# A two-layer hybrid transformer kernel: an order that counts TensorE's instructions, inverse, scan and projections recorded in turns, fewer live tiles, first loads issued at once

## The chip, the cores and the metric

The kernel runs on one core of a Trainium2 chip. A core has five engines that each take their instructions in order: TensorE (PE in the profile; its weight loads are PEld), VectorE (DVE), ScalarE (ACT), GpSimd (POOL) and SyncE (SP), which here issues all DMAs. The metric is device microseconds from the first to the last instruction, as the median of repeated runs; lower is better.

## What is computed

Two layers work on a context stream and a main stream of 256 tokens each, width 1024. Cut to what matters here:

```python
for l in range(2):
    mod = silu(c) @ w_ada[l] + b_ada[l]
    h   = rms_norm(x) * (1 + sc1) + sh1
    q, k, v, z, b, a, u, vg, p, gate = split(h @ w_in[l])
    q, k, v = silu(conv5(q, k, v))
    # per head, direction and chunk: m = strict_lower(beta k k^T decay)
    # sol = (I + m)^-1 rhs ; then a scan over chunks carries the state s
    y_a = norm(o) * silu(z)
    x = x + g1 * (sum(gate_i * (y_i @ w_br_i)) @ w_out)
    x = x + g2 * expert_choice_ffn(rms_norm(x) * (1 + sc2) + sh2)
return rms_norm(x)
```

Eight heads, two directions, both streams; the context's result starts the main stream's scan. The feed-forward part has 16 experts; its weights alone are 192 transfers of 1 MiB in each layer.

## The kernel before, in words

**Recording and ordering.** The program is not written in the order in which it runs. `Net.record` (line 713) calls methods that record operations with their dependences into a `Prog`; `Prog.order` (line 377) then lays them on the engines with a list scheduler, and `emit` (line 609) writes them out. That is why every instruction of the profile carries line 628. Operations are taken by priority (the place in the recording, shifted by `bias`), and only within a window `win` ahead of the oldest one not yet started. `place` (line 407) gives each tile room in one of 25 pages of 2048 words per partition; `give` (line 461) takes it back. `run` (line 701) sets `limits`, the number of tiles of a kind that may live at once (`w` weights as loaded, `hi` their split halves, `wa` modulation weights, `we` expert weights).

**TensorE's two queues.** In the loop of `order` (from line 528 on) matmuls that fill only part of the array (`op.part`) wait in a queue of their own, `ready["tile"]`. That queue goes first if its head is older than the head of the other and full-size matmuls have filled at least `share` of the planner's last `clock` nanoseconds, and once a group is begun (`group[2]`) it goes on first.

**The mixing stage.** `gdn` (line 971) goes over four head pairs `j`. `heads_in` projects, convolves and normalizes k, v and q; `heads_solve` (line 1230) makes the products of keys with decays for both streams (`products`, line 1238) and inverts the chunk matrices (`inverse`, line 1383); `heads_scan` (line 1280) runs the scan. `inverse` works on 32x32 blocks: eight dependent steps (four levels of two) of 64 small matmuls each, then steps for 32 and 64 columns, with a VectorE operation behind each step. A matmul of fp32 operands becomes two matmul instructions and two weight loads, so a step of 64 is 128 of each. `products` loads rows of decays broadcast over the partitions (`rows`), three for a main-stream half, into tiles `R`. Projections (`proj`, line 925) and the other branches (`side`, line 1554) use split operands (fp32r high and low parts, `wsplit`, line 903) and depend little on the scan; `take(n)` records the next `n` of them between solve and scan, as `FILL` says. `Y` and `X64` hold the inverse's result, two sets of each (`NY`).

**The rest.** `ada_in` (line 873) makes the first modulation from 16 weight tiles; the streams are loaded by `record` (line 713), the context first, the main stream after six of the modulation's steps (`XAT`). `merge` and `route` (lines 1591, 1640) end the mixing; `moe` and `expert` (lines 1732, 1782) stream the expert weights.

Of the kernel before, what the change touches and what calls it, by code (L numbers as in the profile page):

```python
# [257 lines left out]
class Prog:  # L258
# [21 lines left out]
    def record(s, eng, fn, a, k):  # L280
# [42 lines left out]
        lim = a[0].tile.lim if isinstance(a[0], View) else None  # L323
        if (not op.deps or eng[0] == "dma") and lim not in ("w", "wa", "we"):
            op.win = min(op.win, 400)
        if lim in ("w", "wa", "we"):
            op.win = 10 ** 9
# [49 lines left out]
    def order(s):  # L377
# [29 lines left out]
        def place(t, spare):  # L407

            up = (t.last - t.first) > 1500 or t.size < 256
            al = 1 << (t.size - 1).bit_length()  # L410
            dt = F32R if t.dt == F32R else F32
            cls = (up, max(al, 256))
            order = range(PAGES - 1, -1, -1) if up else range(PAGES)
            if t.lim == "we":
                order = sorted(order, key=lambda i: freed[i])
            for step in range(3):
                if step == 1 and sum(g is None for g in pages) <= spare:
                    continue
                for i in order:
                    g = pages[i]  # L420
                    if (g is None) != (step == 1) or (g is not None and (g.dt != dt or (step == 0 and g.cls != cls))):
# [39 lines left out]
        def give(t, addr):  # L461
            if t.space == "psum":
                free_banks.append(addr)
                return
            page, a = addr
            b, hs = a + t.size, holes[page.i]
            j = bisect.bisect(hs, (a, b))
            hs.insert(j, (a, b))
            if j + 1 < len(hs) and hs[j + 1][0] == b:
                hs[j:j + 2] = [(a, hs[j + 1][1])]  # L470
            if j > 0 and hs[j - 1][1] == a:
                hs[j - 1:j + 1] = [(hs[j - 1][0], hs[j][1])]
            if hs[0] == (0, PAGE):
                pages[page.i] = None
                turn[0] += 1
                freed[page.i] = turn[0]

# [32 lines left out]
        while left:  # L510
# [17 lines left out]
            for e in engines:  # L528
# [3 lines left out]
                if e == "pe":  # L532
# [3 lines left out]
                    if ready["tile"]:  # L536
                        while recent and recent[0][0] < now - clock:
                            recent.pop(0)
                        much = not span[3] or sum(r[1] for r in recent) < s.limits["share"] * clock
                        queues.append(ready["tile"])  # L540
                        x = ready["tile"][0]
                        if ready[e] and (x < ready[e][0] and not much or group[2]):
                            queues.reverse()
                aside, tries = [], 0
                while queues:
# [26 lines left out]
                    if e == "pe":  # L572
# [57 lines left out]

XAT = 6
CALLS = (-3, -1)
# [24 lines left out]
class Net:  # L657
# [43 lines left out]
    def run(s):  # L701
        tc, t = s.tc, s.t
        limits = dict(w=4, hi=5, wa=5, we=18, fill=0.94, window=800, spare=0, clock=4096 / 1.2, share=0.5, room=ROOM)
        with tc.tile_pool(name="sb", bufs=1) as sb, tc.tile_pool(name="ps", bufs=1, space=PSUM) as ps, \
# [8 lines left out]
    def record(s):  # L713
# [25 lines left out]
        s.xin = [p.tile([128, 2, D], F32, name="xin") for _ in range(2)]  # L739
        nc.sync.dma_start(s.xin[0], s.rows[0].rearrange("(t p) d -> p t d", p=128))  # L740
        s.small = {}
# [10 lines left out]
        for n, _ in enumerate(s.ada_in(0)):  # L752
            if n == EAT:
                s.mark = len(p.ops)
            if n == XAT:
                nc.sync.dma_start(s.xin[1], s.rows[1].rearrange("(t p) d -> p t d", p=128))
        p.bias = LATE
# [115 lines left out]
    def ada_in(s, l):  # L873

        nc, t = s.nc, s.t
        for hf in range(2):
            ps = s.bank("ada")
            for kt in range(8):
                w = s.p.tile([128, 2, 512], F32, name="wada", lim="wa")
                nc.sync.dma_start(w.rearrange("p a b -> p (a b)"), t["w_ada"][l, 0, hf, kt])  # L880
# [90 lines left out]
    def gdn(s, l, ms, side):  # L971
# [21 lines left out]
        take(3)  # L993
        sol = s.heads_solve(ms, 0, qkv[0], Y[0], X[0])
        take(FILL[0])
        for j in range(4):
            p.win = WIN[1]
            o, S, now = {}, None, sol
            for m in ms:
                o[m.k], S = s.heads_scan(m, j, qkv[j][m.k], now[m.k], S)  # L1000
                take(FILL[1])
                if j < 3 and m is ms[0]:
                    sol = s.heads_solve(ms, j + 1, qkv[j + 1], Y[(j + 1) % NY], X[(j + 1) % NY])
                    take(FILL[2])
            while j not in zs:
# [123 lines left out]
    def conv_silu(s, l, units, blk, out):  # L1129
# [3 lines left out]
        for v, bs in units:  # L1133
# [3 lines left out]
            for b in range(nb):  # L1137
# [3 lines left out]
                for tap in (0, 1, 3, 4):  # L1141
# [3 lines left out]
                                             st(acc)[:, :, lo:hi], op0=ALU.mult, op1=ALU.add)  # L1145
                th = s.p.tile([128, n], F32, name="th")
                s.act(th, acc, AF.Tanh, scale=0.5)
# [81 lines left out]

    def heads_solve(s, ms, j, qkv, Y, XF):  # L1230


        MT = [s.p.tile([128, 8, 128], F32, name="MT") for d in range(2)]
        part = {m.k: s.products(m, j, qkv[m.k], [a[:, 4 * z:4 * z + 4, :] for a in MT]) for z, m in enumerate(ms)}
        s.inverse(MT, Y, XF)
        return {m.k: (Y[:, :, 4 * z:4 * z + 4, :],) + part[m.k] for z, m in enumerate(ms)}

    def products(s, m, j, qkv, MT):
# [9 lines left out]
        for i in range(2):  # L1248
            ts = slice(128 * i, 128 * i + 128)
            R = []  # L1250
            for kind in range(3):
                r = None
                if full or kind != 1:
                    r = s.p.tile(B4, F32, name="R")
                    nc.sync.dma_start(r.rearrange("p d h c -> p (d h) c"),
                                      s.bc_rows(s.rowsd[l][k], (kind * 16 + 4 * j) * 256 + 128 * i, [[256, 4], [1, 128]]))
                R.append(r)
# [5 lines left out]
            E = s.p.tile(B4, F32, name="E")  # L1263
            s.tt(E, R[0], s.nb[:, :, None, :].to_broadcast(B4), ALU.add)
# [3 lines left out]
            Eb = s.p.tile(B4, F32, name="Eb")  # L1268
            s.tt(Eb, E, R[2], ALU.mult)
            for d in range(2):  # L1270
                s.tt(MT[d][:, 2 * i:2 * i + 2, :], kq[:, 0], Eb[:, d], ALU.mult)
            if full:
                s.tt(attn[:, i], kq[:, 1][:, None].to_broadcast(B4), E, ALU.mult)
                s.tt(qt[:, i], R[1], qT[:, None, :, ts].to_broadcast(B4), ALU.mult)
        return attn, qt
# [3 lines left out]

    def heads_scan(s, m, j, qkv, sol, S):  # L1280
        nc, k, full, cl = s.nc, m.k, m.full, m.cl
# [9 lines left out]
        for n in range(2):  # L1291
# [38 lines left out]
            if k == 1 and n == 1:  # L1330
                break
            sp2 = s.bank("sp").rearrange("p (d h c) -> p d h c", d=2, h=2)
# [6 lines left out]
            else:  # L1339
                sd = s.p.tile(B4, F32, name="sd")  # L1340
                for d in range(2):
# [4 lines left out]
            S = S2  # L1346
        return o, S

# [34 lines left out]
    def inverse(s, MT, Y, XF):  # L1383
# [21 lines left out]
        for lv in range(1, 5):  # L1405
# [13 lines left out]
            YT = s.p.tile(C4, F32, name="Yc")  # L1419
            V.transpose(flat(YT), flat(X))  # L1420
        for q in range(4):
            s.p.av.copy(units16(Y)[Q[q], :, 32 * q:32 * q + 32], units16(YT)[Q[q]])
# [22 lines left out]
        V.transpose(line(XF[Q[1], 0]), line(yc[Q[0]]))  # L1445
        V.transpose(line(XF[Q[2], 1]), line(yc[Q[3]]))

        H = (slice(0, 64), slice(64, 128))
# [10 lines left out]
        V.tensor_copy(Y[H[0], 0, :, 64:128], yy[H[0]])  # L1459
        V.tensor_copy(Y[H[1], 1, :, 0:64], yy[H[1]])  # L1460

    def chunk_mlp(s, l, ms, rng, yb):
# [390 lines left out]
```

## Time and profile before

| | us |
|---|---|
| median of 3 runs (2397.95 to 2399.71) | 2399.62 |
| the profiled execution, its own time | 2393.84 |
| span of its profile | 2392.1 |
| PE busy in the span | 2041.2 |
| DVE busy | 1122.6 |
| ACT busy | 686.3 |

Busy time is time in which at least one instruction of the engine runs. PEclk (granted clock) is a share of TensorE's full speed: 1.0 is 2.4 GHz, 0.5 is 1.2 GHz. The span falls into a mixing stage (to about 870 us), the experts of layer 0 (to 1312), mixing of layer 1 (to about 1990) and its experts.

### The profile page before, as it was taken

What the parts mean: (1) busy time and instruction counts of PE and PEld (TensorE: products, weight loads), DVE (VectorE), ACT (ScalarE), POOL (GpSimd) and SP (SyncE); (2) the same over time, 40 slices, a digit from 0 to 9 for tenths busy, and PEclk for the clock granted to TensorE, in tenths of its full rate; (3) what the DMA queues carried; (4) which work ended last, traced back from release to release, by engine and by line L of the source; (5) the groups of instructions that cost most, each with busy time, mean ns of one, the idle gap of its engine ahead of it and who ended that gap; (6) DMA issues with size and microseconds to landing.
All of it is one profiled execution on the core that took longest, in us unless ns stands there. A gap on an engine that the chain in (4) does not pass through costs nothing.

```text
span 2392.1 us, 49338 instructions
## 1 busy us (share of the span) xinstructions
PE 2041.2 (85%) x21357; PEld 1344.3 (56%) x21357; DVE 1122.6 (47%) x2478; ACT 686.3 (29%) x1466; POOL 49.3 (2%) x41
## 2 busy tenths in 40 slices
PE   7999989799999989878787899988799976666665
PEld 4877868698779843222222477777799932121111
DVE  4978767664236732212121787666775521010102
ACT  4544436243224420000000455444554410000000
POOL 0000000000000210000000000000000010000000
PEclk9999999899999999999999999898999988887888
DMA  8523314233346599999999743432436989999997
GB/s 292 167 80 110 108 64 138 78 117 106 132 155 232 194 342 421 421 421 421 421 422 421 291 143 119 153 90 69 130 107 214 337 331 421 421 421 421 421 421 308
DMA packets 153906, 602.95 MB, mean 252 GB/s; under 512 B 13948, under 2 KB 60092, under 8 KB 104536
## 3 DMA queue, kind: packets, MB, share of 16 engines
q1 hardware_dynamic: 153688, 599.80, 65.7%
q8 instruction: 167, 2.74, 0.5%
q14 instruction: 51, 0.42, 0.1%
HBM read 597.45 MB, written 2.29 MB: 251 GB/s over the span
## 4 chain that ended last, share of the span: by engine, by line
PE 49%; DMA 36%; DVE 9%; issue 4%; ACT 2%; SPq 0%; DVEq 0%; ACTq 0%
PE bank L628 49%; DMA page<-in_w_up_dram 19%; DMA page<-in_w_down_dram 10%; DVE page L628 9%; DMA page<-in_w_gate_dram 3%; ACT page L628 2%; DMA page<-in_w_in_dram 1%; DMA page<-rows 1%; DMA page<-in_w_ada_dram 1%; DMA page<-in_n_dram 0%; SPq L628 0%; DMA page<-in_b_ada_dram 0%; ACT L628 0%; DVEq L1849 0%; DVEq L628 0%
## 5 line engine op out<-in xcount | busy, mean ns | idle before, releaser
L628 PE MATMUL bank<-page,page 32*32 32x32 f32 (+8 forms) x20611 | 2024.4, 322 | 338.0 <-DVE page L628 99.0
L628 PEld LDWEIGHTS bank<-page,page 32*32 32x32 f32 (+5 forms) x20611 | 1321.4, 143 | 1031.5 <-issue 398.8
L628 ACT ACTIVATE page<-page 128x1024 fp32r<-128x1024 f32 (+7 forms) x485 | 341.4, 719 | 499.3 <-PE bank L628 244.7
L628 DVE TENSOR_TENSOR page<-page,page 128x1024 fp32r<-128x1024 f32 (+3 forms) x471 | 401.5, 876 | 151.7 <-ACT page L628 128.4
L628 ACT ACTIVATE page<-bank 128x512 f32<-128x512 f32 (+5 forms) x332 | 160.2, 497 | 1062.4 <-PE bank L628 1046.4
L628 DVE TENSOR_TENSOR page<-page,bank 128x512 f32<-128x512 f32 (+2 forms) x152 | 96.6, 644 | 578.8 <-ACT page L628 265.7
L628 DVE TENSOR_TENSOR page<-bank,page 128x512 f32<-128x512 f32 (+4 forms) x286 | 147.7, 530 | 283.8 <-PE bank L628 280.5
L628 ACT ACTIVATE page<-page,page 128x128 f32<-128x128 f32 (+2 forms) x388 | 143.9, 435 | 48.4 <-DVE page L628 41.0
L628 DVE SCALAR_TENSOR_TENSOR page<-page,page,page 128x508 f32<-128x508 f32 (+4 forms) x188 | 107.8, 595 | 1.2
L628 DVE COPY page<-bank 128x512 f32<-128x512 f32 (+7 forms) x100 | 52.6, 527 | 36.9 <-PE bank L628 35.4
L628 DVE SCALAR_TENSOR_TENSOR page<-page,page 128x512 f32<-128x512 f32 (+5 forms) x93 | 65.2, 706 | 9.5 <-DMA page<-in_n_dram 7.4
L628 ACT ACTIVATE page<-bank,page 128x256 f32<-128x256 f32 (+2 forms) x85 | 42.0, 516 | 83.3 <-PE bank L628 64.7
L628 DVE SCALAR_TENSOR_TENSOR page<-page,bank 128x512 f32<-128x512 f32 x48 | 32.8, 684 | 60.5 <-PE bank L628 58.4
L628 POOL TENSOR_TENSOR page<-page,page 128x512 fp32r<-128x512 f32 (+1 forms) x16 | 21.2, 1351 | 1915.6 <-ACT page L628 1465.9
L628 DVE TENSOR_SCALAR page<-bank,page 128x128 f32<-128x128 f32 (+3 forms) x65 | 31.2, 496 | 54.5 <-PE bank L628 44.9
L628 DVE TENSOR_TENSOR page<-page 128x4 f32<-128x4 f32 (+3 forms) x301 | 55.2, 197 | 3.3 <-issue 0.3
L628 DVE TENSOR_SCALAR page<-page 128x4 f32<-128x4 f32 (+7 forms) x216 | 37.5, 187 | 25.4 <-ACT page L628 15.6
L628 PE MATMUL bank<-page 32*32 32x32 f32 (+2 forms) x746 | 37.8, 225 | 1.8 <-issue 1.8
L628 DVE TENSOR_SCALAR page<-page,page 128x128 f32<-128x128 f32 (+2 forms) x120 | 37.0, 338 | 2.8 <-PE bank L628 2.0
L628 DVE STREAM_TRANSPOSE page<-page 128x512 f32<-128x512 f32 (+1 forms) x56 | 35.2, 629 | 1.2 <-PE bank L628 0.4
L628 DVE SCALAR_TENSOR_TENSOR page<-bank,page,page 128x128 f32<-128x128 f32 x96 | 29.2, 343 | 10.0 <-PE bank L628 9.9
L628 PEld LDWEIGHTS bank<-page 32*32 32x32 f32 (+2 forms) x746 | 31.1, 133 | 4.4 <-issue 3.2
(23 smaller groups left out, 163.2 us busy)
## 6 DMA issues: line engine op xcount, KB each, us to landing
page<-in_w_gate_dram SPq DMA_DIRECT2D x128, 1024.0 KB, 19.8
page<-in_w_up_dram SPq DMA_DIRECT2D x128, 1024.0 KB, 19.8
page<-in_w_down_dram SPq DMA_DIRECT2D x128, 1024.0 KB, 19.8
page<-in_w_in_dram SPq DMA_DIRECT2D x136, 512.0 KB, 3.9
page<-in_w_ada_dram SPq DMA_DIRECT2D x96, 512.0 KB, 5.3
page<-rows SPq DMA_DIRECT2D x88, 256.0 KB, 5.1
page<-in_w_br_a_dram SPq DMA_DIRECT2D x24, 512.0 KB, 3.6
page<-in_w_out_dram SPq DMA_DIRECT2D x24, 512.0 KB, 4.8
```

The lines of the kernel that those rows point to most:

```text
L628: op.inst = getattr(eng[op.on], fn)(*a, **k)
```

## The change

Five things change. (1) `order` keeps a count of instructions that TensorE may still take before its supply is refilled: `fetch` starts at 320, each operation takes 2 (4 if `op.part`), and 256 come back in 3700 ns of the planner's time. A group of part-array matmuls is begun only when the count is at 250 or more. (2) `gdn` records solve, scan and projections in turns by the string `TURNS`; `heads_solve`, `scans` and `inverse` become generators. (3) Fewer tiles: the decay rows are loaded straight into `E`, `Eb` and `qt`, `th` and `sd` reuse other tiles, `Y` and `X64` have one set (`NY = 1`), `w`, `hi` and `wa` may have 3, 4 and 4 live tiles. (4) `place` goes through the pages of short-lived tiles in the order in which room in them was last given back, and takes an empty page as readily as a partly used one while more than 8 are empty. (5) The 16 first modulation weights get a kind of their own (`wi`, limit 16), and the two streams are loaded after three and seven steps.

```diff
@@ place, give
-            if t.lim == "we":
+            empty = sum(g is None for g in pages)
+            if not up:
                 order = sorted(order, key=lambda i: freed[i])
-            for step in range(3):
-                if step == 1 and sum(g is None for g in pages) <= spare:
+            for step in range(0 if up or empty <= ROOMY else -1, 3):
+                if step == 1 and empty <= spare:
...
@@ order
+        fetch = [CREDIT, 0.0]
...
-                        if ready[e] and (x < ready[e][0] and not much or group[2]):
+                        if group[2]:
+                            fed = fetch[0] + (now - fetch[1]) * REFILL > 0
+                        else:
+                            fed = fetch[0] + (now - fetch[1]) * REFILL >= START
+                        if ready[e] and fed and (x < ready[e][0] and not much or group[2]):
                             queues.reverse()
...
+                        fetch[0] = min(CREDIT, fetch[0] + (now - fetch[1]) * REFILL) - (4 if op.part else 2)
+                        fetch[1] = now
+                        c += max(0.0, -fetch[0] / REFILL)
...
-XAT = 6
+ROOMY = 8
+CREDIT, REFILL, START = 320.0, 256 / 3700.0, 250.0
+XAT = (3, 7)
-FILL = (6, 1, 2)
+FILL = (1,)
+TURNS = ("bsbspbsbsbpbpbpb", "sspssp")
-NY = 2
+NY = 1
-        limits = dict(w=4, hi=5, wa=5, we=18, ...
+        limits = dict(w=3, hi=4, wa=4, wi=16, we=18, ...
@@ gdn
-        sol = s.heads_solve(ms, 0, qkv[0], Y[0], X[0])
-        take(FILL[0])
+        sol = {}
+        for _ in s.heads_solve(ms, 0, qkv[0], Y[0], X[0], sol):
+            take(FILL[0])
         for j in range(4):
             p.win = WIN[1]
-            o, S, now = {}, None, sol
-            for m in ms:
-                o[m.k], S = s.heads_scan(m, j, qkv[j][m.k], now[m.k], S)
-                take(FILL[1])
-                if j < 3 and m is ms[0]:
-                    sol = s.heads_solve(ms, j + 1, qkv[j + 1], Y[(j + 1) % NY], X[(j + 1) % NY])
-                    take(FILL[2])
+            o, now, sol = {}, sol, {}
+            while j < 3 and len(qkv.get(j + 1, ())) < len(ms):
+                take(1)
+            scan = s.scans(ms, j, qkv[j], now, o)
+            solve = s.heads_solve(ms, j + 1, qkv[j + 1], Y[(j + 1) % NY], X[(j + 1) % NY], sol) if j < 3 else iter(())
+            for c in TURNS[j > 2]:
+                if c == "p":
+                    take(1)
+                else:
+                    next(scan if c == "s" else solve, None)
...
@@ products
-            R = []
-            for kind in range(3):
...
+            E, Eb = s.p.tile(B4, F32, name="E"), s.p.tile(B4, F32, name="Eb")
+            for kind, r in enumerate((E, qt[:, i] if full else None, Eb)):
+                if r is not None:
...
-            s.tt(Eb, E, R[2], ALU.mult)
+            s.tt(Eb, E, Eb, ALU.mult)
```

In the orders below a row is a run of equal instructions, out<-in and the output's shape; page and bank numbers only tell tiles apart.

TensorE in the inverse of the second head pair, layer 0: each 32x32 row pair or x64 row is one step of 64; the 128x512 and 128x256 rows are projections. Before:

```order
519 L628 MATMUL bank_67<-page_1229,page_2045 32x32 x64
520 L628 MATMUL bank_66<-page_319,page_2451 128x512
521 L628 MATMUL bank_66<-page_334,page_2451 128x512 x4
522 L628 MATMUL bank_71<-page_2045,page_2339 32x32 x32
523 L628 MATMUL bank_71<-page_2045,page_357 32x32 x32
524 L628 MATMUL bank_66<-page_334,page_2451 128x512 x2
525 L628 MATMUL bank_65<-page_319,page_2451 128x512 x3
526 L628 MATMUL bank_69<-page_1229 32x32 x64
```

Now, from one step to the next of the same inverse (128x128 rows are the scan's and the products'):

```order
593 L637 MATMUL bank_68<-page_879,page_2384 32x32 x64
594 L637 MATMUL bank_65<-page_2603,page_244 128x256
595 L637 MATMUL bank_65<-page_2603,page_237 128x256 x2
596 L637 MATMUL bank_67<-page_2058,page_710 128x128 x4
597 L637 MATMUL bank_71<-page_2058,page_691 128x128
598 L637 MATMUL bank_65<-page_2603,page_244 128x256
599 L637 MATMUL bank_65<-page_2603,page_237 128x256
600 L637 MATMUL bank_65<-page_2660,page_316 128x256 x3
601 L637 MATMUL bank_70<-page_1717,page_91 128x128
602 L637 MATMUL bank_72<-page_879 32x32 x64
```

Where five full-size matmuls stood between two steps, fourteen stand now. Over the eight inverses, 1 to 19 stood between two steps of 64 (median 7), and now 8 to 75 (median 21).

SyncE's queue at the start, with what each load waits for (PE is TensorE's last use of the page; DMAHW is the landing of an earlier transfer on one of eight lanes). Before:

```order
8 L628 DMA page_113<-in_w_ada_dram 128x1024
9 L628 DMA page_113<-in_w_ada_dram 128x1024 [waits DMAHW0_49]
10 L628 DMA page_103<-in_w_ada_dram 128x1024 [waits DMAHW4_49,DMAHW1_49,PE_49]
11 L628 DMA page_103<-in_w_ada_dram 128x1024 [waits DMAHW6_49,DMAHW2_49,PE_49]
12 L628 DMA page_113<-in_w_ada_dram 128x1024 [waits DMAHW7_49,DMAHW3_49,PE_49]
13 L628 DMA page_151<-in_x_dram 128x2x1024 [waits DMAHW5_49]
14 L628 DMA page_113<-in_w_ada_dram 128x1024 [waits DMAHW0_49,PE_49]
```

Now:

```order
8 L637 DMA page_113<-in_ctx_dram 128x2x1024 [waits DMAHW0_49]
9 L637 DMA page_119<-in_w_ada_dram 128x1024 [waits DMAHW1_49]
10 L637 DMA page_119<-in_w_ada_dram 128x1024 [waits DMAHW2_49]
11 L637 DMA page_125<-in_w_ada_dram 128x1024 [waits DMAHW3_49]
12 L637 DMA page_125<-in_w_ada_dram 128x1024 [waits DMAHW4_49]
13 L637 DMA page_138<-in_x_dram 128x2x1024 [waits DMAHW5_49]
14 L637 DMA page_153<-in_w_ada_dram 128x1024 [waits DMAHW6_49]
```

No load of the first modulation waits for TensorE any more; the context comes after three or four of them instead of first. In the whole queue, the loads of `rows` with a wait on TensorE go from 16 of 88 to 26 of 88. TensorE has as many instructions as before, VectorE 15 fewer and ScalarE 11 more, of which four activation table loads are gone. The expert loads stand at the same places of the queue, give or take one.

## Rows read from the trace of the kernel before

**Rows 1.** Page, part 1: busy us (share of the span) xinstructions of each engine.
```profile
PE 2041.2 (85%) x21357; PEld 1344.3 (56%) x21357; DVE 1122.6 (47%) x2478; ACT 686.3 (29%) x1466; POOL 49.3 (2%) x41
```
**Rows 2.** Stages: length; busy us (x) of PE, PEld, DVE, ACT, POOL; PEclk, DMA share, GB/s.
```profile
115.00:480.00 365.00, 327.94 (x6589) 274.37 (x6588) 269.08 (x663) 160.43 (x392) 0.00 (x0) 0.96 0.31 96
1418.00:1750.00 332.00, 288.24 (x6296) 248.69 (x6296) 236.80 (x555) 155.91 (x386) 0.00 (x0) 0.93 0.32 103
...
870.00:1312.00 442.00, 377.76 (x1612) 118.99 (x1610) 80.57 (x117) 12.99 (x20) 4.64 (x5) 1.00 1.01 419
```
**Rows 3.** The same columns, from one inverse to the next, both layers.
```profile
0.00:60.00 60.00, 47.64 (x226) 24.64 (x227) 28.06 (x90) 28.69 (x55) 5.22 (x9) 0.91 0.82 292
...
155.00:225.00 70.00, 69.42 (x502) 57.86 (x501) 61.01 (x169) 42.98 (x128) 0.00 (x0) 1.00 0.46 143
225.00:265.00 40.00, 33.18 (x1322) 28.06 (x1322) 27.05 (x50) 12.18 (x19) 0.00 (x0) 1.00 0.13 42
265.00:325.00 60.00, 57.71 (x414) 50.95 (x413) 47.15 (x123) 28.96 (x87) 0.00 (x0) 1.00 0.42 134
...
367.00:425.00 58.00, 51.07 (x453) 45.46 (x452) 46.90 (x116) 40.03 (x88) 0.00 (x0) 0.98 0.47 136
425.00:480.00 55.00, 47.09 (x1363) 37.80 (x1364) 34.20 (x93) 12.57 (x29) 0.00 (x0) 0.84 0.23 75
...
1458.00:1528.00 70.00, 66.35 (x500) 54.67 (x499) 60.17 (x164) 40.50 (x116) 0.00 (x0) 0.98 0.47 154
1528.00:1575.00 47.00, 39.74 (x1308) 29.70 (x1308) 22.26 (x47) 8.45 (x15) 0.00 (x0) 0.85 0.30 106
1575.00:1630.00 55.00, 52.54 (x377) 46.59 (x376) 46.15 (x118) 39.31 (x105) 0.00 (x0) 0.97 0.36 106
...
1672.00:1708.00 36.00, 30.46 (x275) 29.23 (x275) 32.97 (x93) 31.72 (x79) 0.00 (x0) 0.93 0.65 204
```
**Rows 4.** Groups of PE by form: busy us, mean ns | idle us before, releasers.
```profile
L628 PE MATMUL bank<-page,page 128*128 128x512 f32 x2016 | 526.3, 413 | 10.4 <-DVE page L628 10.2
L628 PE MATMUL bank<-page,page 128*128 128x256 f32 x3400 | 457.5, 291 | 9.4 <-issue 5.1 <-ACT page L628 2.2 <-DVE page L628 2.1
...
L628 PE MATMUL bank<-page,page 32*32 32x32 f32 x8640 | 104.4, 200 | 48.1 <-issue 46.9 <-DVE page L628 1.0
...
L628 PE MATMUL bank<-page 32*32 32x32 f32 x576 | 7.1, 203 | 1.8 <-issue 1.8
```
**Rows 5.** Waits of PE, whole span: us in total, times, longest us.
```profile
PE bank L628 <- issue: 60.1, 57, 3.3
```
**Rows 6.** Single steps of the inverse, stretches as in rows 2.
```profile
118.11:119.32 1.21, 1.21 (x128) 1.17 (x129) 1.19 (x2) 0.10 (x1) 0.00 (x0) 1.00 0.00 0
...
226.72:227.94 1.22, 1.22 (x130) 1.18 (x129) 1.22 (x2) 0.00 (x0) 0.00 (x0) 1.00 0.00 0
229.29:231.58 2.29, 1.44 (x130) 1.28 (x129) 0.78 (x3) 0.00 (x0) 0.00 (x0) 1.00 0.54 191
232.94:235.62 2.68, 1.42 (x130) 1.27 (x129) 0.56 (x2) 1.06 (x1) 0.00 (x0) 1.00 0.00 0
```
**Rows 7.** DMA queue of instructions in 229:265 us: packets, MB, share.
```profile
q8 instruction: 9, 0.15, 1.7%
```
**Rows 8.** The same in 265:325 us.
```profile
q8 instruction: 3, 0.05, 0.3%
```
**Rows 9.** Page, part 3, whole span.
```profile
q8 instruction: 167, 2.74, 0.5%
```
**Rows 10.** Waits of DVE for the broadcast rows, whole span, columns as in rows 5.
```profile
DVE page L628 <- DMA page<-rows: 9.5, 7, 2.3
```
**Rows 11.** Page, part 6: the broadcast rows' loads, KB each, us to landing.
```profile
page<-rows SPq DMA_DIRECT2D x88, 256.0 KB, 5.1
```
**Rows 12.** Waits for the first loads, 0:60 us, columns as in rows 5.
```profile
PE bank L628 <- DMA page<-in_b_ada_dram: 7.9, 1, 7.9
...
PE bank L628 <- DMA page<-in_w_ada_dram: 3.3, 3, 2.8
```

More of the change, by code (lines that the diff above doesn't have):

```diff
@@ L323, in record @@
         lim = a[0].tile.lim if isinstance(a[0], View) else None
-        if (not op.deps or eng[0] == "dma") and lim not in ("w", "wa", "we"):
+        if (not op.deps or eng[0] == "dma") and lim not in ("w", "wa", "wi", "we"):
             op.win = min(op.win, 400)
-        if lim in ("w", "wa", "we"):
+        if lim in ("w", "wa", "wi", "we"):
             op.win = 10 ** 9
@@ L420, in place @@
                     g = pages[i]
-                    if (g is None) != (step == 1) or (g is not None and (g.dt != dt or (step == 0 and g.cls != cls))):
+                    if (step >= 0 and (g is None) != (step == 1)) or (g is not None and (g.dt != dt or (step <= 0 and g.cls != cls))):
                         continue
@@ L472, in give @@
                 hs[j - 1:j + 1] = [(hs[j - 1][0], hs[j][1])]
+            turn[0] += 1
+            freed[page.i] = turn[0]
             if hs[0] == (0, PAGE):
                 pages[page.i] = None
-                turn[0] += 1
-                freed[page.i] = turn[0]
         def release(t):
@@ L702, in run @@
         tc, t = s.tc, s.t
-        limits = dict(w=4, hi=5, wa=5, we=18, fill=0.94, window=800, spare=0, clock=4096 / 1.2, share=0.5, room=ROOM)
+        limits = dict(w=3, hi=4, wa=4, wi=16, we=18, fill=0.94, window=800, spare=0, clock=4096 / 1.2, share=0.5, room=ROOM)
         with tc.tile_pool(name="sb", bufs=1) as sb, tc.tile_pool(name="ps", bufs=1, space=PSUM) as ps, \
@@ L754, in record @@
                 s.mark = len(p.ops)
-            if n == XAT:
-                nc.sync.dma_start(s.xin[1], s.rows[1].rearrange("(t p) d -> p t d", p=128))
+            if n in XAT:
+                k = XAT.index(n)
+                nc.sync.dma_start(s.xin[k], s.rows[k].rearrange("(t p) d -> p t d", p=128))
         p.bias = LATE
@@ L878, in ada_in @@
             for kt in range(8):
-                w = s.p.tile([128, 2, 512], F32, name="wada", lim="wa")
+                w = s.p.tile([128, 2, 512], F32, name="wada", lim="wi" if l == 0 else "wa")
                 nc.sync.dma_start(w.rearrange("p a b -> p (a b)"), t["w_ada"][l, 0, hf, kt])
@@ L993, in gdn @@
         take(3)
-        sol = s.heads_solve(ms, 0, qkv[0], Y[0], X[0])
-        take(FILL[0])
+        sol = {}
+        for _ in s.heads_solve(ms, 0, qkv[0], Y[0], X[0], sol):
+            take(FILL[0])
         for j in range(4):
             p.win = WIN[1]
-            o, S, now = {}, None, sol
-            for m in ms:
-                o[m.k], S = s.heads_scan(m, j, qkv[j][m.k], now[m.k], S)
-                take(FILL[1])
-                if j < 3 and m is ms[0]:
-                    sol = s.heads_solve(ms, j + 1, qkv[j + 1], Y[(j + 1) % NY], X[(j + 1) % NY])
-                    take(FILL[2])
+            o, now, sol = {}, sol, {}
[8 more added lines that the diff above has]
+                    next(scan if c == "s" else solve, None)
+            for g in (scan, solve):
+                for _ in g:
+                    pass
             while j not in zs:
@@ L1228, in keys, with scans, heads_solve @@
         return kt, kT
-    def heads_solve(s, ms, j, qkv, Y, XF):
-        MT = [s.p.tile([128, 8, 128], F32, name="MT") for d in range(2)]
-        part = {m.k: s.products(m, j, qkv[m.k], [a[:, 4 * z:4 * z + 4, :] for a in MT]) for z, m in enumerate(ms)}
-        s.inverse(MT, Y, XF)
-        return {m.k: (Y[:, :, 4 * z:4 * z + 4, :],) + part[m.k] for z, m in enumerate(ms)}
+    def scans(s, ms, j, qkv, sol, o):
+        S = None
+        for m in ms:
+            box = []
+            for _ in s.heads_scan(m, j, qkv[m.k], sol[m.k], S, box):
+                yield 1
+            o[m.k], S = box
+    def heads_solve(s, ms, j, qkv, Y, XF, out):
+        MT = [s.p.tile([128, 8, 128], F32, name="MT") for d in range(2)]
+        part = {}
+        for z, m in enumerate(ms):
+            part[m.k] = s.products(m, j, qkv[m.k], [a[:, 4 * z:4 * z + 4, :] for a in MT])
+            yield 1
+        yield from s.inverse(MT, Y, XF)
+        out.update({m.k: (Y[:, :, 4 * z:4 * z + 4, :],) + part[m.k] for z, m in enumerate(ms)})
     def products(s, m, j, qkv, MT):
@@ L1262, in products @@
                     s.mm(kq[:, 1, h, :], kT[:, h, ts], qT[:, h, ts], True, True)
-            E = s.p.tile(B4, F32, name="E")
-            s.tt(E, R[0], s.nb[:, :, None, :].to_broadcast(B4), ALU.add)
+            s.tt(E, E, s.nb[:, :, None, :].to_broadcast(B4), ALU.add)
             for d in range(2):
@@ L1278, in col, with heads_scan @@
         return lambda i, kind: cl[:, i, kind, 4 * j:4 * j + 4].rearrange("p (d h) -> p d h", d=2)
-    def heads_scan(s, m, j, qkv, sol, S):
+    def heads_scan(s, m, j, qkv, sol, S, out):
         nc, k, full, cl = s.nc, m.k, m.full, m.cl
@@ L1346, in heads_scan @@
             S = S2
-        return o, S
+            yield 1
+        out += [o, S]
     def heads_z(s, l, j, ms):
@@ L1420, in inverse @@
             V.transpose(flat(YT), flat(X))
+            yield 1
         for q in range(4):
@@ L1460, in inverse @@
         V.tensor_copy(Y[H[1], 1, :, 0:64], yy[H[1]])
+        yield 1
     def chunk_mlp(s, l, ms, rng, yb):
```

15 lines of the change are left out of this document (5 added, 10 removed).

## The prediction, made before the changed kernel ran

> **What bounds the kernel now.** I read the busy shares first, then the stages, then single stretches, then the waits inside them. TensorE is busy for 85% of the span, no other engine for half of it [rows 1]. The stages split into two kinds [rows 2]: the experts run at a DMA share of 1.01 and 419 GB/s, so transfers bound them; in the mixing stages the DMA share is 0.31 and 0.32 and TensorE is busy 90% and 87% of 115:480 and 1418:1750. Time won there starts the experts earlier by as much, since the expert loads keep their places in the queue and their 192 transfers their rate.
>
> Where is the idle tenth? In the stretches between two inverses TensorE is nearly full (69.42 of 70 us in 155:225), in those of an inverse it is not (33.18 of 40, 47.09 of 55) [rows 3]. By form, the small 32x32 matmuls are busy for 104.4 + 7.1 us and leave 48.1 + 1.8 us idle before them, of which 46.9 + 1.8 are put down to "issue", that is, to nothing the profile knows [rows 4]; all issue waits of TensorE make 60.1 us [rows 5]. A single step tells why [rows 6]: the first step after a long plain stretch takes 1.21 or 1.22 us for its 128 matmuls, the next ones, a few projections later, 2.29 and 2.68 us for the same work. Meanwhile the queue that carries instructions is at its busiest: 9 packets in the 36 us of an inverse against 3 in the next 60 us [rows 7, 8]. In the whole span it moves 2.74 MB in 167 packets [rows 9]; TensorE has 21357 matmuls and as many weight loads [rows 1], and 2.74 MB over 42714 is 64 bytes each, so this is TensorE's own supply, 256 instructions a packet. An inverse gets 256 every 4 us and can eat the 256 of one step in 1.22. **I read the issue waits as TensorE running out of instructions.**
>
> The Trainium skill (Runtime: NRT & Kernel Launch, Instruction fetch mechanics) says otherwise: fetch is hidden, as an engine's sequencer dispatches more slowly than the supply is refilled. By that rule a count of instructions buys nothing, and the time would be that of the first rival, 2400. The trace speaks against it: the same step runs about twice as fast when it comes rested [rows 6].
>
> **The change, part by part.**
>
> *The count and the turns.* Between two steps of an inverse there now stand 8 to 75 full-size matmuls, median 21, where a median of 7 stood. Most of them cost 457.5 / 3400 = 0.13 to 526.3 / 2016 = 0.26 us [rows 4]. Fourteen, the example in the order, make 1.9 to 3.7 us, which with the step's 1.2 is about the 4 us in which a packet came. So most steps should find their instructions there. First term, idle time: 115:480 and 1418:1750 together hold 697 us, of which TensorE is busy 327.94 + 288.24 = 616.2 and idle 80.8 [rows 2]. What stays idle without the supply's limit I take from the six plain stretches between inverses, which keep all the waits for VectorE, ScalarE and loads: 69.42 + 57.71 + 51.07 + 66.35 + 52.54 + 30.46 = 327.6 busy of 349 us, 6.1% idle [rows 3]. Second term, short stalls that count as busy: 9216 matmuls are 72 steps of 128, at 1.22 us 87.8 us, against 111.5 us busy [rows 4, 6], so 23.7 us at most; a stalled step shows 1.42 to 1.44 busy instead of 1.22 [rows 6], so I take 72 x 0.2, or 14 us. Third, the clock: it is 0.96 and 0.93 in the two windows [rows 2], with 0.84 and 0.85 in stretches full of small, waiting matmuls [rows 3] and 1.00 in 155:225. At most 365 x 0.04 + 332 x 0.07 = 38 us of full-speed work is lost; while TensorE waits for instructions a faster clock gives nothing, so I take 14 us. The new length L follows from L x 0.939 = 616.2 - 14 - 14 = 588, L = 626: **71 us less**. Bounds: nothing (if the waits are not the supply's), and 80.8 + 23.7 + 38 = 142 us less.
>
> Does anything else allow 626 us? VectorE's work there is 269.08 + 236.80 = 506 us, unchanged but for a few operations that ScalarE takes, or 81% of 626. In the plain stretches it runs at 61.01 + 47.15 + 46.90 + 60.17 + 46.15 + 32.97 = 294.4 of 349 us, 84% [rows 3]. It fits, closely. ScalarE has 316 us and four table loads fewer. After the last inverse of each layer hundreds of projections and gates remain as filler, fewer than before, so TensorE doesn't run dry at the end.
>
> *Fewer live tiles, results in place.* No work goes away; results in place add waits of a writer for the last reader. With one `Y` the next inverse's result waits for the scan's reads, and the scan is recorded ahead of it. The decay rows are loaded straight into tiles that VectorE needs soon; one load takes 5.1 us to land [rows 11], and VectorE waited only 9.5 us for them in all [rows 10]. Their loads behind a wait on TensorE go from 16 to 26, and in the order they stand closer to their use. 32 blocks of products are concerned (4 head pairs, 2 streams, 2 halves, 2 layers): bounds nothing and 32 x 5.1 = 163 us of VectorE's waiting. Steps of the inverse come several full-size matmuls after the products, which hides most; I take **5 us more**, nearest to the 9.5 us row. Fewer weight tiles (3 and 4 instead of 4 and 5) lie under the same DMA share of 0.3; I cost them at nothing, with that term's upper part as their bound too.
>
> *First loads.* TensorE is idle for 12.4 of the first 60 us [rows 3], 7.9 of them for the first bias row, which stays; 3.3 us are waits for modulation weights [rows 12], which no longer wait for pages that TensorE must give back. **4 us less**; bounds 0 and 12.4 - 7.9 = 4.5.
>
> *Sum.* -71 + 5 - 4 = -70 us. The profiled execution took 2393.84 us, so it would be about 2324; the median of the timed runs stands 5.8 us above that execution, and against it the forecast is 2399.6 - 70 = **2329 us**.
>
> **The rivals.**
>
> 1. *The count changes nothing.* The issue waits belong to small matmuls as such, however they are spaced. For it: "issue" names no cause. Against it: rested steps run in 1.22 us [rows 6], and packets come at their densest just there [rows 7, 8]. Only first loads and rows are left: 2399.6 - 4 + 5, rounded to 2400. Chance 0.11. (The rule of the Trainium skill's page Runtime: NRT & Kernel Launch would lead here.)
>
> 2. *VectorE takes over.* The chain of an inverse goes through VectorE after every step, and convolutions now sit between. If VectorE sustains only 77% (midway between today's 506 of 697 us, 73%, and the 81% needed), the windows take 506 / 0.77 = 657 us, 40 us less, and with +5 and -4 the time is 2361. For it: the stretches with the best VectorE share hold no inverse. Against it: the extra filler means TensorE needs no quick answer. Chance 0.18.
>
> 3. *Slower: the decay rows come late.* The loads go into tiles whose last reader may be late, and SyncE's queue is in order, so projection weights behind them are late too. Each of the 32 blocks could cost up to 5.1 us [rows 11]. TensorE stands still for it where a step or the products' own matmuls are next in its order. It decides from 70 / 32 = 2.2 us a block beyond what I took; at 3 us a block it is 96 us, and the time 2399.6 - 75 + 96 = 2421. Against it: seven waits in the whole span before. Chance 0.07.
>
> **How the numbers follow.** My forecast has 0.64: around 2329, from 2285 (most of the clock and idle time comes back: -115) to 2350. The range must reach rival 2 and part of the way to no change: **2285 to 2385**. That leaves out rivals 1 and 3 and little else. A measurement of this kernel tells about 0.2%, 5 us, from no change. Faster: 0.64 + 0.18 + 0.04 of rival 1 = 0.86. Same: 0.05 of rival 1. Slower: 0.07 + 0.02 = 0.09.
>
> **What would show it.** Steps of 128 small matmuls near 1.22 us nearly everywhere; TensorE's issue waits well under 20 us instead of 60; instruction packets spread evenly over the mixing stages; TensorE 93 to 95% busy in them, with the clock near 1.00; experts starting some 40 us earlier in layer 0 and 70 in layer 1, at the same rate. I am wrong if issue waits stay though steps are spaced (rival 1), if they go and TensorE waits for VectorE in their place (rival 2), or if waits for the broadcast rows grow to tens of microseconds (rival 3).

## The result, and the profile after

| | before | after |
|---|---|---|
| median, us | 2398.78 (2397.28 to 2399.71, 4 runs) | 2331.55 (2326.93 to 2334.94, 4 runs) |
| ratio to before, 95% interval | | 0.9719 [0.970, 0.9738] |
| span of the profile, us | 2392.1 | 2325.1 |

The forecast was 2329 us, with 2285 to 2385 as its range. The page of the changed kernel, part 1, answers to [rows 1]; its columns are busy time, share of the span and instructions:

```profile
PE 2016.2 (87%) x21357; PEld 1319.7 (57%) x21357; DVE 1121.8 (48%) x2463; ACT 682.0 (29%) x1477; POOL 43.6 (2%) x37
```

The work is the same, but TensorE needs 25.0 us less for it and is idle 42 us less. Where the time went is best read from four marks, the issue of the first and the last expert load of each layer. The timeline of SyncE's queue (start, length) before:

```profile
808.76 0.38 SPq L628 DMA_DIRECT2D page<-in_w_gate_dram  x1
...
1307.78 0.33 SPq L628 DMA_DIRECT2D page<-in_w_down_dram  x1
...
1852.23 0.42 SPq L628 DMA_DIRECT2D page<-in_w_gate_dram  x1
...
2354.96 0.33 SPq L628 DMA_DIRECT2D page<-in_w_down_dram  x1
```

and after:

```profile
775.55 0.38 SPq L637 DMA_DIRECT2D page<-in_w_gate_dram  x1
...
1277.73 0.33 SPq L637 DMA_DIRECT2D page<-in_w_down_dram  x1
...
1789.29 0.42 SPq L637 DMA_DIRECT2D page<-in_w_gate_dram  x1
...
2284.78 0.33 SPq L637 DMA_DIRECT2D page<-in_w_down_dram  x1
```

Layer 0's mixing is 33.2 us shorter; its experts give 3.2 back. Layer 1's mixing (last mark of layer 0 to first of layer 1) takes 511.6 instead of 544.5 us, 32.9 less. Layer 1's expert loads take 7.2 us less, and the tail behind the last of them 40.3 instead of 37.1 us, 3.2 more. The sum is 67.0 us but for rounding, the difference of the spans. So the gain lies in the two mixing stages, and it passes through the expert stages, which run at the rate of before (420 GB/s in 845:1282, 419 in [rows 2]). How it divides between the layers is not fixed: in a second execution of the changed kernel (the control among the experiments, span 2324.8 us) the marks stand at 780.14, 1281.69, 1786.83 and 2285.13, and the mixing stages are 28.6 and 39.3 us shorter than before.

The two mixing stages by stretch. Columns: stretch, length, busy us (instructions) of PE, PEld, DVE, ACT and POOL, then PEclk, DMA share, GB/s. Before, from 10 us to the first expert load, and from 5 us after the last one to the next:

```profile
10.00:808.80 798.80, 751.53 (x8999) 622.17 (x8996) 506.64 (x1150) 337.99 (x711) 6.29 (x4) 0.97 0.41 134
1312.80:1852.20 539.40, 485.82 (x7699) 410.89 (x7700) 387.79 (x904) 262.55 (x594) 0.00 (x0) 0.95 0.44 147
```

After, between the same marks:

```profile
10.00:775.60 765.60, 739.15 (x8991) 610.27 (x8985) 508.57 (x1157) 338.01 (x718) 6.75 (x4) 0.99 0.42 140
1282.70:1789.30 506.60, 475.63 (x7749) 404.68 (x7750) 388.39 (x894) 265.26 (x607) 0.00 (x0) 0.98 0.47 158
```

TensorE's idle time falls from 47.3 + 53.6 to 26.5 + 31.0 us, by 43.4; its busy time from 1237.4 to 1214.8, by 22.6; the clock rises to 0.99 and 0.98. VectorE does the same work in less time.

The stretches of the inverses, which the prediction counted with, stood at 115:480 and 1418:1750 [rows 2]. The inverses now lie in these:

```profile
127.00:490.00 363.00, 345.96 (x6743) 298.03 (x6742) 271.22 (x642) 166.74 (x396) 0.00 (x0) 0.99 0.34 108
1410.00:1712.00 302.00, 280.81 (x6392) 245.79 (x6390) 233.54 (x525) 159.31 (x389) 0.00 (x0) 0.97 0.38 123
```

The small matmuls by form, answering to [rows 4] (busy, mean ns | idle before, releasers):

```profile
L637 PE MATMUL bank<-page,page 32*32 32x32 f32 x8704 | 94.5, 194 | 18.9 <-issue 18.5 <-DVE page L637 0.2
...
L637 PE MATMUL bank<-page 32*32 32x32 f32 x512 | 5.3, 193 | 0.0
```

and the waits of TensorE and VectorE of [rows 5] and [rows 10], us in total, times, longest; the last line is TensorE's waiting for VectorE in the kernel before:

```profile
PE bank L637 <- DVE page L637: 93.6, 89, 5.5
...
PE bank L637 <- issue: 29.1, 29, 4.8
...
DVE page L637 <- DMA page<-rows: 7.0, 4, 2.4
...
PE bank L628 <- DVE page L628: 99.0, 92, 5.5
```

Single steps of the second inverse, as in [rows 6]: some still take 1.74 us, others 1.22. Over all inverses, 42 of the 62 steps of 128 that nothing interrupts take under 1.4 us from the first matmul's start to the last one's end, and 9 take over 2 us; before, it was 15 and 36 of 64.

```profile
242.73:244.47 1.74, 1.43 (x130) 1.28 (x129) 1.07 (x5) 0.00 (x0) 0.00 (x0) 1.00 0.65 177
249.08:250.30 1.22, 1.22 (x130) 1.18 (x129) 0.69 (x1) 1.05 (x3) 0.00 (x0) 1.00 0.05 13
252.78:254.00 1.22, 1.22 (x129) 1.18 (x129) 0.98 (x5) 0.00 (x0) 0.00 (x0) 1.00 0.05 13
```

The queue that carries instructions, in an inverse (239:285) and in the plain 46 us behind it (285:331), as in [rows 7] and [rows 8]:

```profile
q8 instruction: 10, 0.16, 1.5%
...
q8 instruction: 3, 0.05, 0.4%
```

### The profile page after: what moved, and what is told of

The parts are those of the page before. It is cut to its first block, busy times and chain, and to the rows that moved or that the text cites. A ratio compares the mean times of both kernels' runs of the same rounds, so it can differ in the third digit from the quotient of the medians.

```text
span 2325.1 us, 49255 instructions
## 1 busy us (share of the span) xinstructions
PE 2016.2 (87%) x21357; PEld 1319.7 (57%) x21357; DVE 1121.8 (48%) x2463; ACT 682.0 (29%) x1477; POOL 43.6 (2%) x37
## 3 DMA queue, kind: packets, MB, share of 16 engines
HBM read 597.45 MB, written 2.29 MB: 258 GB/s over the span
## 4 chain that ended last, share of the span: by engine, by line
PE 45%; DMA 39%; DVE 10%; issue 3%; ACT 2%; SPq 1%; DVEq 0%; ACTq 0%
PE bank L637 45%; DMA page<-in_w_up_dram 23%; DMA page<-in_w_down_dram 13%; DVE page L637 10%; ACT page L637 2%; DMA page<-in_w_in_dram 1%; DMA page<-rows 1%; DMA page<-in_w_ada_dram 1%; SPq L637 1%; DMA page<-in_n_dram 0%; DMA page<-in_w_out_dram 0%; DMA mod<-page 0%; DVEq L1878 0%; DVEq L637 0%; ACT L637 0%
## 5 line engine op out<-in xcount | busy, mean ns | idle before, releaser
L637 PE MATMUL bank<-page,page 32*32 32x32 f32 (+9 forms) x20676 | 2001.8, 317 | 298.2 <-DVE page L637 93.6
L637 PEld LDWEIGHTS bank<-page,page 128*128 128x128 f32 (+5 forms) x20676 | 1299.1, 139 | 990.9 <-issue 355.2
L637 DVE TENSOR_TENSOR page<-page,page 128x1024 fp32r<-128x1024 f32 (+4 forms) x461 | 395.0, 880 | 132.4 <-ACT page L637 116.8
L637 ACT ACTIVATE page<-page 128x1024 fp32r<-128x1024 f32 (+9 forms) x471 | 334.9, 729 | 411.8 <-DVE page L637 227.4
L637 ACT ACTIVATE page<-page,page 128x128 f32<-128x128 f32 (+3 forms) x413 | 150.5, 431 | 62.8 <-DVE page L637 55.1
L637 DVE COPY page<-bank 128x512 f32<-128x512 f32 (+8 forms) x105 | 55.5, 530 | 64.5 <-PE bank L637 63.8
L637 DVE SCALAR_TENSOR_TENSOR page<-page,page,page 128x128 f32<-128x128 f32 (+4 forms) x156 | 84.2, 565 | 0.9
L637 DVE SCALAR_TENSOR_TENSOR page<-page,page 128x510 f32<-128x510 f32 (+4 forms) x114 | 81.5, 715 | 4.7 <-ACT page L637 2.7
L637 ACT ACTIVATE page<-bank,page 128x128 f32<-128x128 f32 (+2 forms) x94 | 45.2, 506 | 91.2 <-PE bank L637 75.5
L637 DVE TENSOR_SCALAR page<-page 128x4 f32<-128x4 f32 (+6 forms) x212 | 35.9, 179 | 19.3 <-ACT page L637 13.7
```

The costliest lines, as they stand in the source:

```text
L637: op.inst = getattr(eng[op.on], fn)(*a, **k)
```

## The experiments

The theory on trial: in the inverse TensorE runs out of instructions, and the count of instructions, by spacing the steps, is what gives the time. Rivals: the recording in turns, the placement of tiles, or the first loads. All ratios are to the kernel before, timed beside the run in question.

**The disputed cost by itself.** A kernel of its own (it computes nothing of the reference); `full(n)` is n plain 128x256 matmuls. Cut to what matters:

```python
        def step():
            for u in range(16):
                for q in range(4):
                    nc.tensor.matmul(small[Q[q], 32 * u:32 * u + 32], a[Q[q], 32 * u:32 * u + 32],
                                     a[Q[q], 512 + 32 * u:512 + 32 * u + 32], start=True, stop=True)
...
        for n in SPACE:  # 0, 7, 14, 21, 31
            full(240)
            for _ in range(STEPS):  # 16
                step()
                full(n)
```

> Measures the disputed cost by itself and computes nothing of the reference: after 240 plain fp32r 128x256 matmuls, 16 steps of 64 small fp32 32x32 matmuls that wait for nothing, with 0, 7, 14, 21 and 31 plain ones behind each step, five series in one kernel. Supply theory: the first step of a series takes 1.22 us; from the second or third on the step and its plain matmuls together take at least 3.4 to 4 us, so that series 0, 7 and 14 (1.2, 2.2 and 3.1 us if nothing stalled) all take about 3.7 to 4.2 us a step, series 21 (4.0) barely more than 4.0, and series 31 (5.4) shows no stall. Rival (small matmuls stall by themselves, or by their dependences): with no dependences every step takes 1.2 us, or every step 2.3 to 2.7 us, whatever the spacing.

Its five series, each from the start of the first step to the start of the last (columns as above, but without ACT: PE, PEld, DVE, POOL), then single steps: the first of series 0, a later piece of it, and the second of series 7, 14, 21 and 31 each:

```profile
35.26:85.66 50.40, 26.84 (x1922) 25.07 (x1925) 0.00 (x0) 0.00 (x0) 0.57 0.02 5
120.24:173.19 52.95, 38.60 (x2026) 34.40 (x2025) 0.00 (x0) 0.00 (x0) 0.94 0.02 5
205.49:266.30 60.81, 51.59 (x2131) 47.43 (x2130) 0.00 (x0) 0.00 (x0) 0.94 0.02 5
298.96:361.66 62.70, 59.60 (x2236) 56.60 (x2235) 0.00 (x0) 0.00 (x0) 1.00 0.02 4
394.38:473.60 79.22, 77.44 (x2387) 74.49 (x2386) 0.00 (x0) 0.00 (x0) 1.00 0.02 4
...
35.26:36.35 1.09, 1.09 (x130) 1.09 (x132) 0.00 (x0) 0.00 (x0) 1.00 0.00 0
39.57:43.11 3.54, 1.36 (x146) 1.26 (x141) 0.00 (x0) 0.00 (x0) 0.89 0.02 5
122.48:124.84 2.36, 1.41 (x129) 1.26 (x128) 0.00 (x0) 0.00 (x0) 1.00 0.00 0
208.57:210.22 1.65, 1.41 (x129) 1.28 (x129) 0.00 (x0) 0.00 (x0) 1.00 0.00 0
302.88:304.10 1.22, 1.22 (x130) 1.18 (x129) 0.00 (x0) 0.00 (x0) 1.00 0.00 0
399.50:400.72 1.22, 1.22 (x130) 1.18 (x129) 0.00 (x0) 0.00 (x0) 1.00 0.00 0
```

Its DMA queues in 36.35:89.51 (packets, MB, share):

```profile
q8 instruction: 15, 0.25, 1.8%
```

Divided by 15, a step with its plain matmuls takes 3.36, 3.53, 4.05, 4.18 and 5.28 us. Without any stall it would be 1.1, 2.2, 3.1, 3.9 and 5.1: that is how long the first step of each series takes with what follows it, up to the start of the second. So 7 plain matmuls cost next to nothing: the step waits that long anyway. 15 packets in 53.2 us are one in 3.54 us, and a later piece of series 0 takes 3.54 us for little more than a step: **TensorE gets 256 instructions in about 3.5 us.** The first step after a rest takes 1.09 us; nothing in these series waits for data.

Where the waits stand says it most plainly. TensorE's order in series 7 (start, length, idle time before in brackets):

```profile
122.48 1.22 PE L29 MATMUL small<-a 32*32 32x32 f32 x120
124.65 0.26 PE L29 MATMUL small<-a 32*32 32x32 f32 x8 [0.95 <-issue]
124.84 1.09 PE L34 MATMUL plain<-r 128*128 128x256 f32 x7
125.87 1.15 PE L29 MATMUL small<-a 32*32 32x32 f32 x113
128.10 0.32 PE L29 MATMUL small<-a 32*32 32x32 f32 x15 [1.08 <-issue]
```

From one wait to the next there are 8 + 7 + 113 = 128 matmuls, with their weight loads 256 instructions, one packet, and the waits end 3.45 us apart. All 49 issue waits of this kernel stand a whole multiple of 128 matmuls apart, wherever in a step that falls. That settles what "issue" stands for: 7 plain matmuls between steps give 2.36 us, much like the 2.29 of [rows 6], and 21 give 1.22. The rival of small matmuls that stall by themselves falls.

**The count taken out, and the count alone.** Out of the changed kernel:

```diff
...
-                        if ready[e] and fed and (x < ready[e][0] and not much or group[2]):
+                        if ready[e] and (x < ready[e][0] and not much or group[2]):
...
-                        fetch[0] = min(CREDIT, fetch[0] + (now - fetch[1]) * REFILL) - (4 if op.part else 2)
-                        fetch[1] = now
-                        c += max(0.0, -fetch[0] / REFILL)
```

> The changed kernel with the count of instructions taken out of the order; turns, fewer tiles, placement and first loads stay. Between two steps of 64 there stand 2 to 96 full-size matmuls, median 8, as in the kernel before (7), not 21. Supply theory (TensorE runs out of instructions in the inverse): the issue waits come back to 50 to 65 us, and most of the 67 us is lost again: 2375 to 2400 us. Rival turns (the gain is the other work that the turns bring in): 2331 to 2345 us. Rival tiles and placement (waits for pages were what held the order up): 2331 to 2345 us too; the next two runs tell these apart.

and the same lines put into the kernel before:

> The kernel before with the count of instructions added to its order and nothing else. Between two steps of 64 there stand 2 to 268 full-size matmuls, median 19. Supply theory: issue waits of 20 to 35 us as in the changed kernel, and at least half of its gain: 2335 to 2365 us. Rivals turns or tiles and placement: the count alone gives under 10 us, 2390 to 2400 us, or more than 2400 if the steps are only delayed.

Without the count: 2360.5 us, 0.9874 [0.9856, 0.9892]; count alone: 2353.9 us, 0.9843 [0.9826, 0.9859]. TensorE's waits, first without the count:

```profile
PE bank L630 <- issue: 48.1, 46, 4.6
```

then with the count alone:

```profile
PE bank L636 <- DVE page L636: 104.7, 88, 8.5
...
PE bank L636 <- issue: 28.5, 28, 4.1
```

The count alone brings the issue waits to what the changed kernel has (28.5 and 29.1), and 1.57%, about 38 us, as the theory had expected of this run; TensorE waits a little more for VectorE (104.7 us, 99.0 before). The rest of the change without the count brings 1.26%, about 30 us, and takes only 12 us from the issue waits. 1.57% and 1.26% make 2.83%, and the change gives 2.81%: in time the two add up, and the count gives somewhat over half of the gain. For the run without it neither the theory (most is lost) nor its rivals (little is) had foreseen an even split. The mixing stages without the count, between the marks of its own:

```profile
10.00:798.50 788.50, 744.48 (x8988) 617.63 (x8985) 509.94 (x1161) 336.57 (x714) 6.76 (x4) 0.98 0.40 137
1304.80:1822.90 518.10, 478.54 (x7749) 407.31 (x7750) 383.28 (x884) 270.76 (x619) 0.00 (x0) 0.97 0.45 154
```

They are 31.6 us shorter than before, 17.3 of it idle and 14.3 busy time. And with the count alone:

```profile
10.00:792.00 782.00, 743.75 (x8996) 617.52 (x8996) 508.68 (x1163) 334.52 (x705) 6.87 (x4) 0.98 0.41 137
1305.60:1811.40 505.80, 473.58 (x7697) 402.01 (x7698) 390.06 (x904) 262.66 (x594) 0.00 (x0) 0.97 0.46 156
```

They are 50.4 us shorter, 30.4 of it idle and 20.0 busy time. So inside these stages the two don't add up: 50.4 and 31.6 make 82.0, and the whole change takes 66.0 off. With the count alone 9.5 us are lost again between the first and the last expert load of layer 0 (508.5 us instead of 499.0); why is open.

**Which part carries the other half?** Undone one at a time, in the changed kernel. The old order of recording, at first with one `Y`: the main stream's scan then reads the inverse of the next head pair, which is a different computation, with other dependences.

```diff
-TURNS = ("bsbspbsbsbpbpbpb", "sspssp")
+TURNS = ("sspbbbbbbbbppssp", "sspssp")
...
-            take(FILL[0])
+            pass
+        take(6)
```

> The changed kernel with the recording in turns undone (scan of the context, whole solve, scan of the main stream, as before); count, tiles, placement and first loads stay. Median 18 full-size matmuls between steps. Supply theory: the count finds its filler without the turns, 2331 to 2350 us. Rival turns: 2380 us or more.

2360.4 us, 0.986 [0.9844, 0.9877], between the two expectations. With the other dependences this says little of the turns. So again with `NY = 2`, as before the change:

> The changed kernel with two sets of Y and X64 again and the old order of recording (context's scan, next solve, main stream's scan, projections by 6, 2 and 1); count, placement, reused tiles and first loads stay. What the count left unexplained in the runs without it and with it alone is about 28 us. Theory turns (the other half is the interleaved recording): about 2355 us, as with the count alone, with TensorE waiting more for VectorE. Rival placement (pages reused in the order of release take false waits away): within 8 us of the changed kernel, 2325 to 2340 us.

2345.8 us, 0.9794 [0.977, 0.9818], between what the two theories had expected. The old placement:

> The changed kernel with the old rule of placement (partly used pages first, in order of their number). Theory turns: within 8 us of the changed kernel, 2325 to 2340 us. Rival placement: 2345 to 2360 us, with more loads and writers waiting for pages.

2349.2 us, 0.9817 [0.9792, 0.9842], where the rival had put it. The old first loads (`XAT` and the limit of the first weights as before):

> The changed kernel with the first loads as before: the context's stream first, the main stream after six steps of the modulation, and the first modulation weights under the limit of 4 live tiles. My term for the first loads: 4 us slower, 2330 to 2340 us, with the experts of layer 0 starting 2 to 6 us later. Rival (the start is bound elsewhere): no difference. Rival (the first loads carry the other half): 2350 us or more.

2339.3 us, 0.9784 [0.9761, 0.9808], in the expected range; but the experts of layer 0 start at 787.0 us, 11.4 us later than in the profiled execution of the changed kernel and 6.8 later than in its second one, where 2 to 6 were expected. And an edit meant to help, the count made exact:

```diff
+            op.n = 2 if acc[2][0].dtype == F32R else 4
...
-                        fetch[0] = min(CREDIT, fetch[0] + (now - fetch[1]) * REFILL) - (4 if op.part else 2)
+                        fetch[0] = min(CREDIT, fetch[0] + (now - fetch[1]) * REFILL) - op.n
```

> The changed kernel with the count made exact: full-size fp32 matmuls and transposes of fp32, which become more than one matmul and weight load, take 4 from the count and not 2. The supply series showed 256 instructions in 3.5 us and steps of 1.22 us once 21 plain matmuls stand between. Supply theory: the 29 us of issue waits that are left fall to 10 to 25 us, and the time by 3 to 15 us, 2315 to 2330 us. Rival (what is left of issue waits is not the supply's): no difference, 2327 to 2337 us.

2341.3 us, 0.9783 [0.9758, 0.9808], with 33.1 us of issue waits instead of 29.1: a miss. Four unlike edits had each lost 0.6 to 1%. That called for a control, and for edits that mean nothing.

> The changed kernel unaltered, as a control beside the next three on the same chip. Ratio to before 0.970 to 0.974, as measured.

> The changed kernel with one number of the planner that has nothing to do with any part of the change (the margin it adds for a result on its way into TensorE) at 57 instead of 60 ns, so that the list scheduler falls into another order. Theory shares (each part of the change carries its share, the undone ones showed it): within 5 us of the changed kernel. Theory picked order (the changed kernel's order is a lucky one among its neighbours, and any small edit loses something): 6 to 20 us slower.

> The same with 63 ns. Theory shares: within 5 us of the changed kernel. Theory picked order: 6 to 20 us slower, so that the 8 to 20 us of the runs with a part undone tell little of that part.

> The kernel before with the same nudge to 63 ns. If orders scatter by 6 to 20 us, this one is 5 to 20 us slower than the kernel before (which would be a picked one as well), or within 5 us of it if the kernel before lies in the middle of its neighbours. Supply theory: in either case it stays above 2370 us, with issue waits of 50 to 70 us.

| | median, us | ratio, 95% interval | issue waits, us |
|---|---|---|---|
| changed kernel again | 2327.6 | 0.9737 [0.9712, 0.9762] | 27.4 |
| 57 instead of 60 ns | 2333.0 | 0.9758 [0.9732, 0.9784] | 29.7 |
| 63 instead of 60 ns | 2342.7 | 0.9795 [0.9772, 0.9818] | 40.6 |
| kernel before, 63 ns | 2390.1 | 0.9998 [0.9981, 1.0016] | 55.1 |

A nudge that has nothing to do with the change goes with a loss of 0.2 to 0.6%, 5 to 15 us; the smaller one lies within the intervals, and the kernel before shows none. So the 0.5 to 0.8% lost with the turns, the loads or the placement undone can't be put down to these parts; only the placement's 0.9817 lies above every nudge, and its interval still overlaps with that of the worst. What stands outside the scatter that these three nudges show is the count (0.9874 without it) and the sum of the other parts (0.9843 with the count alone). **How the other 30 us divide among turns, tiles, placement and first loads stays open**, and so does how much of them is the luck of one order among many.

## Why the prediction was right, point by point

- **What bounds it.** Right. The mixing stages shrank by 33.2 and 32.9 us (28.6 and 39.3 in the second execution; about 40 and 30 were forecast), and the gain reached the end one to one, as the sum took it. "Nearly full" between inverses was read from the best of six stretches: 367:425 and 1672:1708 are idle for 12% and 15% [rows 3]. The 6.1% takes them in.
- **Issue waits are TensorE's supply.** Right, and shown by the supply kernel: a packet in 3.5 us, and all waits whole packets apart. I had read 4 us from an inverse of the old trace, which had plain matmuls and other waits in it. The rule of the Trainium skill (Runtime: NRT & Kernel Launch, Instruction fetch mechanics), that fetch is hidden, does not hold for these small matmuls: a step takes 128 matmuls and 128 loads in 1.22 us and gets 256 in 3.5.
- **Term 1, idle time.** I had 80.8 us falling to 6.1% of 626, or 38 us. In 127:490 and 1410:1712, the same stretches now, TensorE is idle for 17.0 + 21.2 = 38.2 us, and between the marks idle time fell by 43.4. The size is right, though not its make-up: I expected issue waits well under 20 us, and 29.1 are left. Nor are the stretches 626 us long: they are 665 and hold more matmuls (13135 against 12885). The time came off behind the last inverses instead: from there to the first expert load it is 285.6 and 77.3 us now (490:775.6, 1712:1789.3), where it was 328.8 and 102.2 (480:808.8, 1750:1852.2). Steps well behind enough plain matmuls still wait now and then: series 31 of the supply kernel takes 5.28 us a step where 5.1 would be free of stalls, and in the changed kernel one wait lasts 4.8 us. What is left is still the supply: 22 of the 29 waits, 25.1 us of the 29.1, stand whole packets of 128 matmuls apart but for a slow drift (the matmul's number, divided by 128, leaves 88 at first and 43 some 16850 matmuls later), as 49 of the 57 did before. The other seven, 0.56 us each, stand in the experts of layer 1, in both kernels at the same matmuls. Why the planner's count still lets packets run out, and why one wait lasts 4.8 us, is open; the exact count did not mend it.
- **Terms 2 and 3, short stalls and clock.** I took 14 + 14 us; busy time fell by 22.6 us. The small matmuls' part is 111.5 - 99.8 = 11.7 us. The clock's cannot be read apart, but PEclk rose from 0.97 and 0.95 to 0.99 and 0.98.
- **VectorE fits.** Right: it holds 508.57 of 765.6 and 388.39 of 506.6 us, and TensorE's waits for it went from 99.0 to 93.6 us. Rival 2 did not come.
- **Tiles in place and rows.** Waits for the broadcast rows went from 9.5 to 7.0 us, so the 5 us that I added were not there. Rival 3 did not come.
- **First loads.** TensorE is busy for 50.70 us of the first 60 against 47.64 [rows 3], 3 us where I took 4. That is not shown to be theirs: other runs with the same first loads have 49.32 (the control), 48.57 (without the count) and 47.43 (old placement), and the one with the old loads 48.90. The 5 us that I added for the rows and the 4 that I took off here did not show; that they nearly cancel, and left the sum unharmed, is luck.

```profile
0.00:60.00 60.00, 50.70 (x237) 24.68 (x237) 31.63 (x107) 26.84 (x54) 2.92 (x7) 0.94 0.83 315
```

- **Signs.** Of those that I named, "1.22 us nearly everywhere" (42 of 62 steps), issue waits well under 20 us and packets spread evenly (10 in 46 us of an inverse, 3 in the 46 behind it) did not come.
- **The step that was too coarse** is "The count and the turns": I priced them as one term and explained it by the spacing alone. Spacing by itself gave about 38 us; some 30 came from the rest of the change, of which 12 show in the issue waits. The sum held because the bound that I used, idle time as between the inverses, does not ask which edit gets there.

## What to carry to other kernels

When TensorE waits for "issue" and its matmuls are tiny, count its instructions: compare how fast it eats a packet's worth with how often packets of the instruction queue arrive. If the matmuls at which it waits stand whole packets apart, it is the supply. Put plain matmuls between bursts until burst and filler last about as long as a packet takes; they are nearly free there (in the supply kernel 7 of them added 0.2 us to a step, 21 added 0.8 us and did 2.7 us of work). And when a list scheduler writes the order, nudge a number that means nothing before you believe that an edit of half a per cent did something.

## What the runs showed of the hardware that was not expected

- TensorE's clock fell to half (1.2 GHz) while it had nothing but small matmuls to run and waited for instructions alone: 0.57 on average in series 0 of the supply kernel and 0.50 late in it, 0.94 in the series with 7 and with 14 plain matmuls, 1.00 in those with 21 and 31. In this kernel, then, where instructions were missing the clock was lost as well; that this is how busy time came down in the changed kernel fits its PEclk, but wasn't tried by itself. The late piece of series 0:

```profile
82.83:86.30 3.47, 1.67 (x125) 1.54 (x119) 0.00 (x0) 0.00 (x0) 0.50 0.00 0
```

- The supply did not slow at half clock: series 0 and series 7 took 3.36 and 3.53 us a step with clocks of 0.57 and 0.94.
